# Two placements for the split weights of a column pair, and the order of their products

## The chip, the core and the metric

The kernel runs on one core of one Trainium2 chip. The metric is device time in microseconds of one execution. Engines by their names in the profile: PE (matrix products), PEld (loading of the stationary operand into PE), DVE (vector), ACT (scalar and activation), POOL, SP (here: issue of DMAs).

## The reference, cut to what matters

Two transformer blocks on 256 tokens of width 1024, all in float32. Block one: a modulated RMS norm, a mixer with three attention branches whose gated outputs are merged, and a convolutional feed-forward layer of width 2816. Block two: a gated linear attention layer, then a dilated sliding-window attention layer, each with a layer norm.

```python
z = h @ w_in                                    # q, k, v of three branches, gates zg
gates = jax.nn.sigmoid(zg.reshape(B_, S, 3, 1024) + b_gate)
merged = sum(gates[:, :, i] * (y_i @ w_branch[i]) for i in range(3))
x = x + g1 * _rmsnorm(merged @ w_out, ...)
a, g = jnp.split(h2 @ w_up, 2, axis=-1)         # feed-forward: 5632 columns
x = x + g2 * _rmsnorm((jax.nn.gelu(conv(a)) * g) @ w_down, ...)
q, k, v, g, a_lr = jnp.split(x @ gla_w_in, ...) # linear attention
k, v = jnp.split(x3 @ w_kv, 2, axis=-1)         # shared keys and values
q, g = jnp.split(x3 @ swa_w_in, [3072], axis=-1)
```

Every product is float32 x float32, and nearly all of the weights (some 35 million numbers) are used once, for all 256 tokens.

## The kernel before

**Products in three parts.** PE runs its fast float32 form (`F32R`) on operands that are split into a high and a low part. A weight piece of 128 x 1024 goes from HBM into a tile `raw` (DMA on SP's queue), ACT copies it to `whi` (line 158) and DVE writes the remainder into `wlo` (line 159). Activations are split in the same way (`hhi`/`hlo`, `h2hi`/`h2lo`, `x2hi`/`x2lo`, `x3hi`/`x3lo`). `mm3` (line 271) then issues three products into one accumulator: low weights with high activations, high weights with low activations, high with high. All of them are recorded at line 262.

**Two ways round.** In `tokmm` the activations are stationary and the weights stream by, 512 columns at a time; these chunks (`out`, `dn`, `gvg`, `gout`, `kvv`, `sout`) are not touched by the change. In `wpair` (line 522) and in the first loop (line 493) the weights are stationary and the 256 tokens stream by: each product loads one 128 x 128 block of weights and streams 128 x 256 of activations. A `wpair` chunk holds two column tiles of 128 outputs, each with 8 blocks along the contraction, so 2 x 8 x 3 = 48 products. Column tile 0 is the first piece of the chunk (`parts[0]`), column tile 1 the second; they go to the two halves of one PSUM tile. All of tile 0 comes first, then tile 1. `fresh` chunks (the first `up` and the first `kvk`) have an order of their own.

**Places in memory.** `whi` and `wlo` have six buffers each, so three chunks. A `whi` tile has 4096 bytes a partition; a `wlo` tile has 4224, and for the keys in `STILL` (all weights that are stationary) its data begins 64 bytes in. So high parts begin at 0 and low parts at 64 modulo 128, in both pieces. Activations lie in `big8` tiles (line 397), whose last argument shifts the data by that many floats: 0 for `hhi`, `hlo`, `x2hi`, `x2lo`, `h2hi`; 16 (64 bytes) for `h2lo`; 8 and 24 (32 and 96 bytes) for `x3hi` and `x3lo`.

**Order.** `Stream.get` (line 168) hands out a chunk and issues the DMA and the conversion of the chunk two further on; those pieces wait until their buffers are free, that is, until the last product that reads them is done. Each engine works off its instructions in order. That order is made when the program is built, by a list scheduler that takes what is ready by its own cost model and by priorities that follow the program (`tc.high_priority(n)` moves work ahead, `issue_after` holds it behind another instruction). So an edit can also move neighbours.

**Stages, in microseconds of the profile.** First projections `in1` (18 to 66); gates `zg` and branches `br` mixed with the three attentions (66 to 190); `out` (190 to 213); feed-forward `up` and `dn` (221 to 406); linear attention with `gla`, `gk` (410 to 438) and then `gvg`, `gout`; shared keys and values `kvk`, `kvv` (543 to 577); eight heads of window attention with two `sq` chunks each (577 to 703); the end. In `in1` each of eight steps holds 12 column tiles of one block, 8 in piece 0 and 4 in piece 1.

Of the kernel before, what the change touches and what calls it, by code (L numbers as in the profile page):

```python
# [20 lines left out]
KK = 8  # L21
# [11 lines left out]
SC_SWA = float(128.0 ** -0.5)  # L33


STILL = ("in1", "inc", "zg", "br", "up", "gla", "gk", "kvk", "sq")

COLS = {}

# [63 lines left out]
class Stream:  # L103
# [31 lines left out]
    def _chunk(self, i):  # L135
        nc = self.nc
        key, ap, n, part = self.items[i]
        if part < 0:
            raw = self.early.tile([128, n], F32, tag="early", name="early", bufs=3)
        else:  # L140
            raw = self._raw()
        if not part:
            for o in range(0, n, 1024):
                nc.sync.dma_start(raw[:, o:o + 1024], ap[:, o:o + 1024])
            self.done.append(raw)
            return
        nc.sync.dma_start(raw[:, :n], ap)
        parts = []
        for o in range(0, n, part) if part > 0 else range(0, -part, 1024):
            m = min(part, n - o) if part > 0 else min(1024, -part - o)  # L150
            hi = self.pool.tile([128, 1024], F32R, tag="whi", name="whi", bufs=self.hlbufs)
            lo = self.pool.tile([128, 1056], F32R, tag="wlo", name="wlo", bufs=self.hlbufs)
            lo = lo[:, 16:1040] if key[0] in STILL else lo[:, 0:1024]
            with ExitStack() as st:
                for ins in self.behind:
                    st.enter_context(self.tc.issue_after(ins))
                st.enter_context(self.tc.high_priority(self.pri))
                i0 = nc.scalar.activation(hi[:, :m], raw[:, o:o + m], AF.Copy)  # L158
                i1 = nc.vector.tensor_sub(lo[:, :m], raw[:, o:o + m], hi[:, :m].bitcast(F32))  # L159
                self.last = (i0.ins, i1.ins)  # L160
            parts.append((hi, lo))
        self.done.append((part, parts) if part > 0 else (raw, (1024, parts)))
# [36 lines left out]
def wsl(w, a, b):  # L199

    part, parts = w
    i = a // part
    assert b <= (i + 1) * part
    return tuple(t[:, a - i * part:b - i * part] for t in parts[i])
# [26 lines left out]
def hybrid_blocks(ctx, tc, A, out, dbg=None):  # L231
# [29 lines left out]
    def mm(o, l, r, start, stop, share=False):  # L261
        return pe.matmul(o, l, r, start=start, stop=stop, skip_group_check=share)  # L262
# [5 lines left out]
            st.enter_context(tc.issue_after(i))  # L268
        return st

    def mm3(o, l, r, start, stop, share=False):
        mm(o, l[1], r[0], start, False, share)
        mm(o, l[0], r[1], False, False, share)
        return mm(o, l[0], r[0], False, stop, share)

    def sl(pair, *ix):
        return tuple(t[ix] for t in pair)
# [215 lines left out]
    for j in range(KK):  # L493
        cur = h32
        ws.behind = at
        raw, w = ws.get(("in1", j), 1 if j + 1 < KK else None)
        if j + 1 < KK:
            h32, at = first_h(j + 1, gemv(ws.get(("ada", j + 1), 0))[0])
        h = sl(hT, slice(None), j, slice(None))
        for n in range(8):  # L500
            o = qk[n // 4][n % 4 // 2][:, (n % 2) * 256:(n % 2 + 1) * 256]
            mm3(o, wsl(w, n * 128, (n + 1) * 128), h, j == 0 and n % 2 == 0, j == KK - 1, True)
        for n in range(4):
            o = qci[n // 2][:, (n % 2) * 256:(n % 2 + 1) * 256]
            mm3(o, wsl(w, 1024 + n * 128, 1024 + (n + 1) * 128), h, j == 0 and n % 2 == 0, j == KK - 1, True)
        for b in range(2):
            mm(vps[b], cur[:, b * 128:(b + 1) * 128], raw[:, 1536:2048], j == 0, j == KK - 1)
    ws.pri = 0
# [8 lines left out]
    def wstat(o, w, base, a, share=False, kk=KK):  # L517
        for k in range(kk):
            mm3(o, wsl(w, base + k * 128, base + (k + 1) * 128), sl(a, slice(None), k, slice(None)),
                k == 0, k == kk - 1, share)  # L520

    def wpair(key, a, fresh=False):


        w = ws.get(key)
        p = mm_t()
        if fresh:
            for n in range(2):
                o = p[:, n * 256:(n + 1) * 256]
                W = [wsl(w, n * 1024 + k * 128, n * 1024 + (k + 1) * 128) for k in range(KK)]  # L530
                for k, l in enumerate(W):
                    mm(o, l[1], a[0][:, k, :], k == 0, False)
                    mm(o, l[0], a[0][:, k, :], False, False)
                for k, l in enumerate(W):
                    mm(o, l[0], a[1][:, k, :], False, k == KK - 1)
            return p
        for n in range(2):
            wstat(p[:, n * 256:(n + 1) * 256], w, n * 1024, a)
        return p

    def rope_pair(wk, tag, p, ctab, stab, half, dst, n=2, nb=2, scale=1.0):
# [360 lines left out]

    close_p1()
    close_p1a()
    res, _ = open_pool("res")
    ctx.callback(_)
    p2, close_p2 = open_pool("p2")
    wk = p2
    xn = p2.tile([128, 2, D], F32, name="xn")
# [281 lines left out]
    xqt = p3.tile([128, 2, D], F32, name="lnw", tag="sg")  # L1191
    layer_norm(x2, y3, row("lng0"), None, x3, lambda i: (xkt, xqt)[i // 2][:, i % 2, :], ORD3)
    dump("x3", x3)
    x3T = (big8(F32R, "x3hi", 8), big8(F32R, "x3lo", 24))

    def ev_x3(j, p, act, dve):
        for low in range(2):
# [16 lines left out]
            nc.scalar.dma_start(x3d[b], x3[:, b, :])  # L1214

    close_p3()
    p4, close_p4 = open_pool("p4")
    ctx.callback(close_p4)
    wk = p4
# [224 lines left out]
```

## Time and profile before

| | us |
|---|---|
| median of 3 runs | 741.2 (741.21, 735.28, 741.20) |
| the profiled execution | 733.62 |
| its span, first to last instruction | 731.6 |
| PE busy in the span | 700.6 (96%) |
| PEld busy | 636.4 (87%) |
| DVE busy | 547.1 (75%) |
| ACT busy | 407.1 (56%) |
| mean granted clock of PE | 0.986 |

A product's record on PE is longer than the distance to the next one, because products overlap in the pipeline; busy time of PE is the union of the records and therefore says only that PE had something under way. What a product costs in a stream is the distance from its start to the next start. In the rows, `mm<-x3hi,wlo` means that the moving operand is `x3hi`, the stationary one `wlo`, and the output a PSUM tile named `mm`.

### The profile page before, as it was taken

The page shows a single profiled execution, that of the slowest core. Times are in us where ns is not written, and L with a number is a line of the kernel's source. Part 1 is how long each engine was busy: PE and PEld are TensorE (multiplying, and loading weights), DVE is VectorE, ACT ScalarE, POOL GpSimd, SP SyncE. Part 2 cuts the span into 40 slices and gives each one's busy share as a digit, 9 for nine tenths or more (in the row PEclk, how much of TensorE's full clock was granted, in tenths as well). Part 3 has the DMA queues.
Part 4 walks back from the last instruction along what each step waited for, and adds up shares of the span by engine and source line. Part 5 has one row for each costly group of instructions (what it writes and reads, how often), then busy time and mean ns, then how long its engine had stood idle before and what let it go on. Part 6 is the DMA issues. An engine that isn't in the chain of part 4 may idle for free. (4 is left out here: it accounts for less than half of the span.)

```text
span 731.6 us, 12192 instructions
## 1 busy us (share of the span) xinstructions
PE 700.6 (96%) x4878; PEld 636.4 (87%) x4878; DVE 547.1 (75%) x933; ACT 407.1 (56%) x675; POOL 20.2 (3%) x34
## 2 busy tenths in 40 slices
PE   4999999999979999999999899999989999999995
PEld 4888888998859999998999797888879999999984
DVE  5877969898868776768566756675777689777866
ACT  3447788546548555554545774543555556555542
POOL 0001000000010000000000200001010000000000
PEclk8999999999999999999999999999999999999999
DMA  8996768677734765758554464231437755433201
GB/s 321 418 345 237 275 257 301 229 250 255 256 136 174 276 243 178 262 207 310 201 195 174 181 224 141 109 116 58 189 142 276 261 194 168 168 125 135 89 1 57
DMA packets 24600, 148.74 MB, mean 203 GB/s; under 512 B 2992, under 2 KB 3248, under 8 KB 9568
## 3 DMA queue, kind: packets, MB, share of 16 engines
q1 hardware_dynamic: 21888, 139.05, 52.1%
q0 software_dynamic: 1280, 5.18, 2.1%
q10 hardware_dynamic: 1376, 3.74, 1.5%
q8 instruction: 38, 0.62, 0.3%
q14 instruction: 18, 0.15, 0.1%
HBM read 145.86 MB, written 2.10 MB: 202 GB/s over the span
## 5 line engine op out<-in xcount | busy, mean ns | idle before, releaser
L159 DVE TENSOR_TENSOR wlo<-raw,whi 128x1024 fp32r<-128x1024 f32 (+1 forms) x193 | 231.3, 1210 | 63.1 <-ACT whi L158 63.1
L158 ACT ACTIVATE whi<-raw 128x1024 fp32r<-128x1024 f32 (+1 forms) x193 | 199.4, 1050 | 94.1 <-PE acc L262 42.5
L262 PE MATMUL mm<-h2hi,wlo 128*128 128x256 f32 x352 | 98.3, 280 | 0.0
L262 PE MATMUL mm<-h2hi,whi 128*128 128x256 f32 x352 | 98.1, 280 | 0.0
L262 PE MATMUL mm<-h2lo,whi 128*128 128x256 f32 x352 | 97.0, 282 | 0.0
L262 PE MATMUL mm<-x3hi,wlo 128*128 128x256 f32 x304 | 86.2, 285 | 0.0
L262 PE MATMUL mm<-x3hi,whi 128*128 128x256 f32 x304 | 85.1, 281 | 0.0
L262 PE MATMUL mm<-x3lo,whi 128*128 128x256 f32 x304 | 82.9, 280 | 0.0
L262 PEld LDWEIGHTS mm<-h2hi,wlo 128*128 128x128 f32 x352 | 67.0, 190 | 0.4
L262 PEld LDWEIGHTS mm<-h2hi,whi 128*128 128x128 f32 x352 | 66.9, 190 | 0.0
L262 PEld LDWEIGHTS mm<-h2lo,whi 128*128 128x128 f32 x352 | 65.1, 188 | 0.3
L262 PE MATMUL mm<-hhi,wlo 128*128 128x256 f32 x208 | 59.5, 286 | 0.5 <-DVE wlo L159 0.3
L262 PE MATMUL mm<-hlo,whi 128*128 128x256 f32 x208 | 59.2, 285 | 0.0
L262 PE MATMUL mm<-hhi,whi 128*128 128x256 f32 x208 | 58.7, 282 | 0.0
L262 PEld LDWEIGHTS mm<-x3hi,wlo 128*128 128x128 f32 x304 | 57.7, 190 | 0.0
L262 PEld LDWEIGHTS mm<-x3hi,whi 128*128 128x128 f32 x304 | 57.5, 189 | 0.0
L262 PEld LDWEIGHTS mm<-x3lo,whi 128*128 128x128 f32 x304 | 56.2, 188 | 0.0
L262 PEld LDWEIGHTS mm<-hhi,wlo 128*128 128x128 f32 x208 | 39.0, 188 | 2.5 <-PE mm L262 0.8
L262 PEld LDWEIGHTS mm<-hlo,whi 128*128 128x128 f32 x208 | 39.1, 188 | 0.8 <-issue 0.8
L262 PEld LDWEIGHTS mm<-hhi,whi 128*128 128x128 f32 x208 | 39.1, 188 | 0.6 <-issue 0.5
L445 DVE SCALAR_TENSOR_TENSOR adacc<-raw,cact,adacc 128x1024 f32<-128x1024 f32 x28 | 35.7, 1276 | 0.2
L262 PE MATMUL acc<-whi,flo 128*128 128x512 f32 x88 | 34.8, 395 | 0.0
(355 smaller groups left out, 1604.0 us busy)
## 6 DMA issues: line engine op xcount, KB each, us to landing
raw<-in_w_up_dram SPq DMA_DIRECT2D x22, 1024.0 KB, 4.9
raw<-in_w_ada_dram SPq DMA_DIRECT2D x16, 1024.0 KB, 4.9
raw<-in_swa_q_dram SPq DMA_DIRECT2D x16, 1024.0 KB, 4.9
raw<-in_w_zg_dram SPq DMA_DIRECT2D x12, 1024.0 KB, 4.9
raw<-in_w_dn_dram SPq DMA_DIRECT2D x11, 1024.0 KB, 4.7
raw<-in_w_ada_dram SPq DMA_DIRECT2D x16, 512.0 KB, 9.0
early<-in_w_in_dram SPq DMA_DIRECT2D x8, 1024.0 KB, 7.3
raw<-in_gla_vg_dram SPq DMA_DIRECT2D x8, 1024.0 KB, 5.1
```

The costliest lines, as they stand in the source:

```text
L158: i0 = nc.scalar.activation(hi[:, :m], raw[:, o:o + m], AF.Copy)
L159: i1 = nc.vector.tensor_sub(lo[:, :m], raw[:, o:o + m], hi[:, :m].bitcast(F32))
L262: return pe.matmul(o, l, r, start=start, stop=stop, skip_group_check=share)
L445: dve.scalar_tensor_tensor(a, w, c, a, op0=OP.mult, op1=OP.add)
```

## The change

`STILL` is split. For seven of its nine keys (`ALTERNATE`) the place now depends on the piece: in even pieces the high part begins at 0 and the low part at 64 modulo 128, in odd pieces it is the other way round. `whi` tiles grow to 4224 bytes for that. `br` and `gla` stay as they were. In `wpair`, apart from `fresh`, the loop over the two column tiles moves inside the loop over the contraction, and the three products of a block go as high weights with low activations, low weights with high activations, high with high (`turn`). The first loop takes its 12 column tiles in the order 0, 1, 2, 3, 4, 8, 5, 9, 6, 10, 7, 11, also with `turn`. `x3hi` and `x3lo` lose their shifts. The pool `res`, which holds `x2`, is closed before the pool `p4` of the last stage opens, rather than at the end.

```diff
--- before.py
+++ after.py
@@ -33,7 +33,9 @@
 SC_SWA = float(128.0 ** -0.5)
 
 
-STILL = ("in1", "inc", "zg", "br", "up", "gla", "gk", "kvk", "sq")
+
+ALTERNATE = ("in1", "inc", "zg", "up", "gk", "kvk", "sq")
+STILL = ALTERNATE + ("br", "gla")
 
 COLS = {}
 
@@ -148,9 +150,11 @@
         parts = []
         for o in range(0, n, part) if part > 0 else range(0, -part, 1024):
             m = min(part, n - o) if part > 0 else min(1024, -part - o)
-            hi = self.pool.tile([128, 1024], F32R, tag="whi", name="whi", bufs=self.hlbufs)
+            hi = self.pool.tile([128, 1056], F32R, tag="whi", name="whi", bufs=self.hlbufs)
             lo = self.pool.tile([128, 1056], F32R, tag="wlo", name="wlo", bufs=self.hlbufs)
-            lo = lo[:, 16:1040] if key[0] in STILL else lo[:, 0:1024]
+            odd = len(parts) % 2 if key[0] in ALTERNATE else 0
+            past = (16 * odd, 16 * (1 - odd)) if key[0] in STILL else (0, 0)
+            hi, lo = (t[:, p:p + 1024] for t, p in zip((hi, lo), past))
             with ExitStack() as st:
                 for ins in self.behind:
                     st.enter_context(self.tc.issue_after(ins))
@@ -268,10 +272,11 @@
             st.enter_context(tc.issue_after(i))
         return st
 
-    def mm3(o, l, r, start, stop, share=False):
-        mm(o, l[1], r[0], start, False, share)
-        mm(o, l[0], r[1], False, False, share)
-        return mm(o, l[0], r[0], False, stop, share)
+    def mm3(o, l, r, start, stop, share=False, turn=False):
+
+        for n, (i, j) in enumerate(((0, 1), (1, 0), (0, 0)) if turn else ((1, 0), (0, 1), (0, 0))):
+            ins = mm(o, l[i], r[j], start and n == 0, stop and n == 2, share)
+        return ins
 
     def sl(pair, *ix):
         return tuple(t[ix] for t in pair)
@@ -497,12 +502,9 @@
         if j + 1 < KK:
             h32, at = first_h(j + 1, gemv(ws.get(("ada", j + 1), 0))[0])
         h = sl(hT, slice(None), j, slice(None))
-        for n in range(8):
-            o = qk[n // 4][n % 4 // 2][:, (n % 2) * 256:(n % 2 + 1) * 256]
-            mm3(o, wsl(w, n * 128, (n + 1) * 128), h, j == 0 and n % 2 == 0, j == KK - 1, True)
-        for n in range(4):
-            o = qci[n // 2][:, (n % 2) * 256:(n % 2 + 1) * 256]
-            mm3(o, wsl(w, 1024 + n * 128, 1024 + (n + 1) * 128), h, j == 0 and n % 2 == 0, j == KK - 1, True)
+        for n in (0, 1, 2, 3, 4, 8, 5, 9, 6, 10, 7, 11):
+            o = (qk[n // 4] if n < 8 else qci)[n % 4 // 2][:, (n % 2) * 256:(n % 2 + 1) * 256]
+            mm3(o, wsl(w, n * 128, (n + 1) * 128), h, j == 0 and n % 2 == 0, j == KK - 1, True, True)
         for b in range(2):
             mm(vps[b], cur[:, b * 128:(b + 1) * 128], raw[:, 1536:2048], j == 0, j == KK - 1)
     ws.pri = 0
@@ -534,8 +536,10 @@
                 for k, l in enumerate(W):
                     mm(o, l[0], a[1][:, k, :], False, k == KK - 1)
             return p
-        for n in range(2):
-            wstat(p[:, n * 256:(n + 1) * 256], w, n * 1024, a)
+        for k in range(KK):
+            for n in range(2):
+                mm3(p[:, n * 256:(n + 1) * 256], wsl(w, n * 1024 + k * 128, n * 1024 + (k + 1) * 128),
+                    sl(a, slice(None), k, slice(None)), k == n == 0, k == KK - 1, True, True)
         return p
 
     def rope_pair(wk, tag, p, ctab, stab, half, dst, n=2, nb=2, scale=1.0):
@@ -902,8 +906,7 @@
 
     close_p1()
     close_p1a()
-    res, _ = open_pool("res")
-    ctx.callback(_)
+    res, close_res = open_pool("res")
     p2, close_p2 = open_pool("p2")
     wk = p2
     xn = p2.tile([128, 2, D], F32, name="xn")
@@ -1191,7 +1194,7 @@
     xqt = p3.tile([128, 2, D], F32, name="lnw", tag="sg")
     layer_norm(x2, y3, row("lng0"), None, x3, lambda i: (xkt, xqt)[i // 2][:, i % 2, :], ORD3)
     dump("x3", x3)
-    x3T = (big8(F32R, "x3hi", 8), big8(F32R, "x3lo", 24))
+    x3T = (big8(F32R, "x3hi"), big8(F32R, "x3lo"))
 
     def ev_x3(j, p, act, dve):
         for low in range(2):
@@ -1214,6 +1217,7 @@
             nc.scalar.dma_start(x3d[b], x3[:, b, :])
 
     close_p3()
+    close_res()
     p4, close_p4 = open_pool("p4")
     ctx.callback(close_p4)
     wk = p4
```

## Rows read from the trace of the kernel before

**Rows 1.** The page: its first line, and busy time, share of the span and instructions of PE and DVE.

```profile
span 731.6 us, 12192 instructions
PE 700.6 (96%) x4878; PEld 636.4 (87%) x4878; DVE 547.1 (75%) x933; ACT 407.1 (56%) x675; POOL 20.2 (3%) x34
```

**Rows 2.** The waits of PE: who waited for whom, us in total, times, longest. The first row is the longest of all; the second is the only one for weights.

```profile
PE acc L890 <- DVE x L193: 4.1, 3, 2.7
...
PE mm L262 <- DVE wlo L159: 0.3, 1, 0.3
```

**Rows 3.** Busy time by stage: stretch, its length, then busy us (and instructions) of PE, PEld, DVE, ACT, POOL, the granted clock, the share of the DMA engines and GB/s.

```profile
18.00:66.00 48.00, 48.00 (x317) 39.68 (x316) 38.76 (x73) 23.14 (x38) 1.65 (x3) 0.96 0.87 330
66.00:190.00 124.00, 121.26 (x992) 111.75 (x991) 111.58 (x232) 85.46 (x182) 2.01 (x3) 1.00 0.73 268
...
577.00:703.00 126.00, 125.98 (x995) 122.27 (x994) 100.51 (x185) 74.54 (x121) 0.00 (x0) 1.00 0.41 142
```

**Rows 4.** The chain that ended last, in order of time: start, us, what. The last stages, from 410 on; a piece of 48 is one `sq` chunk.

```profile
410.41 6.28 PE mm L262 x49
...
646.57 5.67 PE mm L262 x48
```

**Rows 5.** Groups of instructions by line and shape: the products of stationary weights with 256 tokens, one group of each three; count, busy us, mean ns of one record, idle before.

```profile
L262 PE MATMUL mm<-h2hi,wlo 128*128 128x256 f32 x352 | 98.3, 280 | 0.0
...
L262 PE MATMUL mm<-x3hi,wlo 128*128 128x256 f32 x304 | 86.2, 285 | 0.0
...
L262 PE MATMUL mm<-hhi,wlo 128*128 128x256 f32 x208 | 59.5, 286 | 0.5 <-DVE wlo L159 0.3 <-DVE st L674 0.2
...
L262 PE MATMUL mm<-x2hi,wlo 128*128 128x256 f32 x72 | 20.4, 284 | 0.0
```

**Rows 6.** Timeline of PE in a gate chunk: start, us of the record, what. Consecutive products; three rows are one block.

```profile
83.00 0.28 PE L262 MATMUL mm<-hlo,whi 128*128 128x256 f32 x1
83.12 0.28 PE L262 MATMUL mm<-hhi,whi 128*128 128x256 f32 x1
83.23 0.28 PE L262 MATMUL mm<-hhi,wlo 128*128 128x256 f32 x1
83.35 0.28 PE L262 MATMUL mm<-hlo,whi 128*128 128x256 f32 x1
83.47 0.28 PE L262 MATMUL mm<-hhi,whi 128*128 128x256 f32 x1
83.58 0.28 PE L262 MATMUL mm<-hhi,wlo 128*128 128x256 f32 x1
83.69 0.28 PE L262 MATMUL mm<-hlo,whi 128*128 128x256 f32 x1
```

**Rows 7.** Timeline of PE, first and last start of low weights with high activations in five stretches of back-to-back products: the `inc` chunk (15 such rows), a gate chunk (15), two `up` chunks (32), the second and third `gk` (19 of theirs), three of `sq` (46).

```profile
66.74 0.28 PE L262 MATMUL mm<-hhi,wlo 128*128 128x256 f32 x1
...
71.59 0.28 PE L262 MATMUL mm<-hhi,wlo 128*128 128x256 f32 x1
...
131.85 0.28 PE L262 MATMUL mm<-hhi,wlo 128*128 128x256 f32 x1
...
136.84 0.28 PE L262 MATMUL mm<-hhi,wlo 128*128 128x256 f32 x1
...
293.63 0.28 PE L262 MATMUL mm<-h2hi,wlo 128*128 128x256 f32 x1
...
304.39 0.28 PE L262 MATMUL mm<-h2hi,wlo 128*128 128x256 f32 x1
...
418.89 0.28 PE L262 MATMUL mm<-x2hi,wlo 128*128 128x256 f32 x1
...
425.24 0.28 PE L262 MATMUL mm<-x2hi,wlo 128*128 128x256 f32 x1
...
577.87 0.28 PE L262 MATMUL mm<-x3hi,wlo 128*128 128x256 f32 x1
...
593.79 0.28 PE L262 MATMUL mm<-x3hi,wlo 128*128 128x256 f32 x1
```

**Rows 8.** Timeline of PE in a `dn` chunk, the other way round (activations stationary, 512 columns of weights stream by): first and last of 8 starts of `wlo` with `fhi`, with two products between each.

```profile
288.40 0.40 PE L262 MATMUL acc<-wlo,fhi 128*128 128x512 f32 x1
...
293.18 0.39 PE L262 MATMUL acc<-wlo,fhi 128*128 128x512 f32 x1
```

**Rows 9.** Timelines of PE and DVE where a chunk starts before its second piece is converted: the first product of the gate chunk, then the conversion of its second low part. Two gate chunks; then the four low parts of `gk` 0 and 1 in one row.

```profile
107.10 0.38 PE L262 MATMUL mm<-hhi,wlo 128*128 128x256 f32 x1
...
108.43 1.22 DVE L159 TENSOR_TENSOR wlo<-raw,whi 128x1024 fp32r<-128x1024 f32 x1
...
156.15 0.35 PE L262 MATMUL mm<-hhi,wlo 128*128 128x256 f32 x1 [0.29 <-DVE wlo L159]
...
156.32 1.21 DVE L159 TENSOR_TENSOR wlo<-raw,whi 128x1024 fp32r<-128x1024 f32 x1
...
412.08 4.63 DVE L159 TENSOR_TENSOR wlo<-raw,whi 128x1024 fp32r<-128x1024 f32 x4
```

**Rows 10.** Timeline of ACT in the feed-forward: the high parts of the two pieces of `up` 11, each when its buffer comes free.

```profile
296.62 1.06 ACT L158 ACTIVATE whi<-raw 128x1024 fp32r<-128x1024 f32 x1 [1.73 <-PE mm L262]
...
299.86 1.05 ACT L158 ACTIVATE whi<-raw 128x1024 fp32r<-128x1024 f32 x1
```

## The prediction, made before the changed kernel ran

> **What bounds the kernel now.** I read the page first, then the waits of PE, then busy time by stage, then the chain. PE has something under way for 96% of the span, and DVE, the next engine, for 75% [rows 1]. The longest single wait of PE is 4.1 us in total, and for converted weights it waited once, 0.3 us [rows 2]. In the window attention PE is busy 125.98 of 126 us [rows 3], and the chain of work that ended last runs there through product after product, one `sq` chunk being 5.67 us of it [rows 4]. So from the feed-forward on, a shorter product is a shorter kernel. Two stages are less simple. In the first 18 to 66 us the DMA engines are 87% busy at 330 GB/s [rows 3]: weights arrive no faster than that, and what PE saves there it waits for again. From 66 to 190 us DVE is busy 111.58 of 124 us beside PE's 121.26 [rows 3], with the attentions' vector work and the conversions in one queue.
>
> Busy PE is not PE at its peak, so the question is what one product costs in a stream. I take distances between starts. In a gate chunk [rows 6] the step after low activations with high weights is 0.12 to 0.13 us (83.00, 83.35 and 83.69 to the next start), the other two kinds 0.11 to 0.12. All three stream 256 columns. A block of weights is loaded while the product before it streams (PEld is busy 636.4 us beside PE, [rows 1]). The long step is the one during which the next block lies at the same place modulo 128 as the block before it (high after high); during the other two the place changes. Over whole stretches [rows 7], three products take (71.59 - 66.74)/14 = 346 ns in the `inc` chunk, (136.84 - 131.85)/14 = 356 in a gate chunk, (304.39 - 293.63)/31 = 347 in `up`, (425.24 - 418.89)/18 = 353 in `gk` and (593.79 - 577.87)/45 = 354 in `sq`. Same instructions, same clock, two levels about 8 ns apart.
>
> **How low can it go?** The bound comes from `dn` [rows 8]: 21 products of 512 columns between 288.40 and 293.18, 227.6 ns each. There a load comes only once in 512 columns, and still a column costs the same as in the short steps above: half of 227.6 is 113.8, three times that 341.4. I take this as the floor of three products.
>
> One page of the Trainium skill would put it lower: "TensorE: Matmul & The Clock Gate" (section Back-to-back issue gap) gives columns over 2.4 GHz plus 2.5 ns, by my estimate 109 ns for 256 columns. No row here shows a product of this form that short, and by it the sum below would be some 12 us larger.
>
> **The change, part by part.**
>
> *Placement and turns.* High, low, high of one column tile now lie at 0, 64, 0, the next at 64, 0, 64, so each load changes place against the one before. If the reading above is right, all three products step at the floor. Triples per stage, from counts [rows 5]: `up` has 352, less 16 in the `fresh` chunk: 336 x (347 - 341.4) = 1.9 us. `sq` is 16 chunks, 256 triples of the 304: 256 x 12.6 = 3.2 us; two `kvk` chunks, 32 x 12.6 = 0.4 us. `gk` is 64 of the 72: 64 x 11.6 = 0.7 us. The gates and `inc` are 208, between the two levels; at their middle, 351, this is 208 x 9.6 = 2.0 us. Together 8.2 us. The bounds of this term: nothing below the floor, so 8.2 (9.2 if all gate chunks were at 356) is the top; at the bottom each step could become like the long one (0.123 by [rows 6], 370 ns per triple), bounded below under the rivals. I take the upper part, because the steps with changing places are short in [rows 6], which is the nearest row.
>
> *`in1`.* Its 96 triples are behind the DMA engines [rows 3]: nothing. If weights came early, the price would be 96 x 5 ns = 0.5 us.
>
> *Both pieces at the start.* Column tile 1's low part is now wanted at the fifth product, some 0.47 us into the chunk (four steps of 0.12), no longer after half of it (2.8 us by the 5.67 of [rows 4]). Where conversion is ahead this costs nothing. Where it is not [rows 9]: one gate chunk starts at 107.10 and its second low part is ready at 108.43 + 1.22 = 109.65, so PE would stand until then, 2.1 us; part of that is filled by score products that now follow, and I take 1.0. Another starts at 156.15, second low part ready 157.53: 0.9 us. `gk` 0 starts after the 24 `gla` products, near 413.2 [rows 4], with its second low part ready at 412.08 + 4.63/2 = 414.4: 0.7 us. Together 2.6; between 0 (the list scheduler puts other products there) and 3.7. Queued behind such a product are PE's attention products, and behind these ACT's and DVE's softmax.
>
> *Buffers come free later.* Piece 0 used to be released at half time: `up` 11's first high part starts 3.24 us before its second [rows 10]. Now both start at the end of a chunk. They are wanted two chunks later, more than 11 us (2 x 5.5) against 3.5 us of two ACT and two DVE conversions at 1.06 and 1.22 [rows 9, 10]: nothing, as long as the two engines are free. The cover is the third buffer; in the gates, where DVE is 90% busy, it may fail, which the 3.7 above includes.
>
> *Places of x3, larger `whi`, `res` closed early.* `x3hi` and `x3lo` at 0 are placed as `hhi` and `hlo`, whose chunks have shown both levels [rows 7]; no price of its own. The last stage's tiles move in memory; x2's last reader is the first layer norm, long before, so no new wait; I bound it by 0.5 us either way.
>
> **The sum.** 8.2 - 2.6 = 5.6, rounded up to 6 us for waits that the scheduler fills. The profiled execution took 733.62 us (span 731.6 and 2.0 around it), so some 727.7 there, 0.8% less. The median of the runs is 741.2, 1% above the profiled one; the same 0.8% makes 735.
>
> **Rivals.**
>
> *Place doesn't matter.* The two levels also occur with the same places: `hhi`, `hlo` in the two chunks of [rows 7], and `x2` is placed like `h` but stays at 353. So the level may be a rhythm between load and stream that any order can fall into. Then the triples stay where they are, and only the waits are left: 741.2 + 0 to 3.7, near 743. Against it: within one chunk the long step is always the same one [rows 6]. The Trainium skill's page "SBUF — State Buffer" (section SBUF: two separate sides) would have it so, since it gives PE one read port for the moving operand and a second, independent one for weights. Rows 6 do not agree with two ports that never meet.
>
> *The new order is worse.* Slower by this: the turns give load and stream no step in which they get clear of each other, and each step becomes the long one, 123 ns or 370 per triple. The `up` chunks, whose `h2lo` at 64 is placed for the old order, pay most: 336 x 23 = 7.7 us; `sq`, `kvk` and `gk` 352 x 16 = 5.6; the gates 208 x 19 = 4.0. That is 17 us and 758 at the extreme; it is slower by 1% from a mean of 362 per triple (896 triples, 8 ns more, 7.4 us). For it: no trace shows this order. Against it: even the worst stretch shows 356.
>
> *The floor is not one.* Steps fall under 113.8, to 110 say: 896 x 11 = 10 us more, 725. For it: the floor is read from another form. Against it: not one row below it.
>
> *Half of it.* Only activations at equal places gain, `up` stays at 347: 1.9 less, 737. It lies within the range.
>
> **Chances.** Forecast, a gain of 3.5 to 9 us (732 to 738, half of it included): 0.55. Place doesn't matter, within 1%: 0.22. Worse order: 0.14. No floor: 0.09. A difference of 1% (7.4 us) is about what a measurement of this kernel can tell from none, as its own three runs lie 0.8% apart. Faster by over 1% takes the whole of no-floor and two fifths of the forecast, as 8.2 us without waits is 1.1%: 0.09 + 0.22 = 0.31. Slower by over 1%: 0.14. Within: 0.55. The range leaves out the worse order beyond 744 and the far end of no-floor: 727 to 744.
>
> **What the profile after would show.** If right: in `sq` and `gk`, three products within 345 ns, the three kinds of step equal, a `sq` chunk near 5.45 us in the chain; in `up` the same or 347 still. DVE's low parts of odd pieces as PE's releaser in the gates, 1 to 3 us in all. ACT's two conversions back to back at a chunk's end in the feed-forward, with no wait of PE behind. It would be wrong if `sq` chunks stay at 5.67, or if the waits for `wlo` come to more than the products save.

## The result and the profile after

The changed kernel takes 744.5 us (median of 7 runs, 744.0 to 746.1) against 736.7 us (735.3 to 741.2) of the kernel before (median of 7 runs): a ratio of 1.0105, interval 1.008 to 1.013. It is slower by about 1%, where 735 us were predicted and a range of 727 to 744. The prediction counted from 741.2, the median of the three runs it had; in its own terms a gain of 6 us was forecast and a loss of 7.8 came. The profiled execution took 744.11 us with a span of 742.1, 10.5 us more than the span of before [rows 1].

The page of the kernel after, its first line and the busy times:

```profile
span 742.1 us, 12200 instructions
...
PE 706.3 (95%) x4878; PEld 641.1 (86%) x4878; DVE 545.2 (73%) x933; ACT 405.6 (55%) x675; POOL 20.2 (3%) x34
```

PE has the same 4878 product records and is busy 5.7 us longer. The other 4.8 us are gaps. Where the time is lost is seen from the start of each stage's unbroken run of products in the two timelines:

| starts at (us) | before | after | lost in the stage before it |
|---|---|---|---|
| `inc`, first gate products | 66.4 | 66.3 | -0.1 |
| `out` | 191.4 | 196.5 | 5.2 |
| `up` | 220.5 | 226.2 | 0.6 |
| x2 into `gla` | 410.4 | 419.0 | 2.9 |
| `kvk` | 542.8 | 551.5 | 0.1 |
| `sq` | 577.2 | 586.3 | 0.4 |
| `sout`, the end | 700.1 | 710.6 | 1.4 |

Three of them lost: the gates, the feed-forward and the window attention. The 0.6 us before `up` belong to the gates too: in the kernel before, two products of `out` ran early, at 189.4, which in the kernel after are still to be done at 196.5. For the gates and the window attention, the waits of PE in the kernel after (who waited for whom: us in total, times, longest), beside [rows 2]:

```profile
PE mm L266 <- DVE wlo L163: 3.7, 4, 1.8
...
PE mm L266 <- ACT th L747: 1.8, 2, 1.2
...
PE at L1286 <- DVE sP L1273: 1.0, 3, 0.3
```

The first row was 0.3 us before; the other two are new. Against them, two waits for `Pat` on ACT fell from 2.0 to 0.4 us. The longest wait in the timeline of the kernel after: PE's last product, DVE's conversion that it is waiting for, and the product that follows.

```profile
86.30 0.28 PE L266 MATMUL mm<-hlo,whi 128*128 128x256 f32 x1
...
87.08 1.22 DVE L163 TENSOR_TENSOR wlo<-raw,whi 128x1024 fp32r<-128x1024 f32 x1
...
88.36 0.44 PE L266 MATMUL mm<-hhi,wlo 128*128 128x256 f32 x1 [1.78 <-DVE wlo L163]
```

This is the low part of a second piece, wanted at the fifth product of a gate chunk, as the prediction said; only it is another chunk than the two it priced. Windows of the kernel after for the gates, for the window attention and for two short stretches inside the gates (columns as in [rows 3]; the granted clock is the third number from the end):

```profile
66.00:196.00 130.00, 124.37 (x997) 115.53 (x996) 112.35 (x232) 86.29 (x182) 2.02 (x3) 0.97 0.70 256
586.00:713.00 127.00, 126.04 (x993) 121.97 (x992) 98.56 (x183) 73.36 (x120) 0.00 (x0) 1.00 0.40 141
...
88.55:91.96 3.41, 3.41 (x18) 3.41 (x17) 2.74 (x11) 2.96 (x6) 0.00 (x0) 0.50 0.77 245
132.93:136.34 3.41, 3.41 (x18) 3.41 (x17) 3.41 (x8) 2.00 (x2) 0.00 (x0) 0.50 0.90 303
```

In the gates PE is without work for 5.6 of 130 us, after 2.7 of 124 [rows 3]. The granted clock is 0.97 there, after 1.00: in the two short stretches it is at the lower of its two levels, 1.2 GHz, and products step at 213 ns instead of 118, which loses some 1.7 and 1.5 us. The first begins right behind the wait above, the second with no wait of that length before it. The traces of `order_only` and `narrow_turns` below, which have the same turns, show both at the same points of the gates; that of the kernel before has none in the gates. But `x3_64` and `shift_128`, in the old order, have one each, near 134. So part of the gates' loss is clock, and the timed runs below measure waits and clock together.

For the feed-forward, the timeline of PE in the kernel after: the first and last of 32 starts of `wlo` with `h2hi` in two `up` chunks, and of 48 starts with `x3hi`, as in [rows 7].

```profile
283.64 0.28 PE L266 MATMUL mm<-h2hi,wlo 128*128 128x256 f32 x1
...
294.63 0.28 PE L266 MATMUL mm<-h2hi,wlo 128*128 128x256 f32 x1
...
586.43 0.28 PE L266 MATMUL mm<-x3hi,wlo 128*128 128x256 f32 x1
...
603.04 0.28 PE L266 MATMUL mm<-x3hi,wlo 128*128 128x256 f32 x1
```

(294.63 - 283.64)/31 = 354.5 ns per triple in `up`, 347 before: 336 x 7.5 = 2.5 of the 2.9 us; the rest is `dn`, whose three products went from 684 to 688 ns (88 x 4 ns = 0.4). (603.04 - 586.43)/47 = 353.4 in `sq`, 354 before. Nowhere do three products take 341. In the chain of waits a `sq` chunk has 5.66 us (5.67 in [rows 4]):

```profile
663.25 5.66 PE mm L266 x48
```

### The profile page after: what moved, and what is told of

The parts are those of the page before. It is cut to its first block, busy times and chain, and to the rows that moved or that the text cites. A ratio compares the mean times of both kernels' runs of the same rounds, so it can differ in the third digit from the quotient of the medians.

```text
span 742.1 us, 12200 instructions
## 1 busy us (share of the span) xinstructions
PE 706.3 (95%) x4878; PEld 641.1 (86%) x4878; DVE 545.2 (73%) x933; ACT 405.6 (55%) x675; POOL 20.2 (3%) x34
## 5 line engine op out<-in xcount | busy, mean ns | idle before, releaser
L266 PE MATMUL mm<-hlo,whi 128*128 128x256 f32 x208 | 61.6, 296 | 0.0
L266 PEld LDWEIGHTS mm<-hhi,wlo 128*128 128x128 f32 x208 | 40.6, 195 | 4.6 <-DVE wlo L163 4.1
```

## The experiments

In what follows `up`, `x2` and x3 stand for the mean triple in two `up` chunks, over the last 55 starts of `wlo` in `gk`, and in the first three chunks of `sq`, worked out from first and last starts as above. Ratios are against the kernel before, run beside each kernel on the same chip. The later groups rest on the addresses that the built program gives to the tiles; no trace shows them. In the kernel before, `whi` buffers lie 4096 bytes apart, all at 0 modulo 256. Its `wlo` buffers, 4224 bytes apart, put the low parts at 64 and 192 by turns, and its `up` chunks are at 347 with either. The two buffers of the activations lie at 0 (`hhi`, `h2hi`, `x2lo`, `x3hi`) and at 128 modulo 256 (`hlo`, `h2lo`, `x2hi`, `x3lo`), to which the shifts are added. Places modulo 128, as the section on the kernel before gives them, hide that.

### Streams by themselves

One kernel without loads or conversions in between: streams of 96 products each, in the orders and at the places modulo 128 of before and after, and some simpler ones.

```diff
+STREAMS = [
...
+    ('sa', 'tiles', (0, 16, 0, 16), (0, 0)),
...
+    ('sg', 'turns', (0, 16, 16, 0), (0, 16)),
...
+    ('sj', 'turns', (0, 16, 0, 16), (0, 16)),
...
+    ('tc', 'w_alt', (0, 16, 0, 0), (0, 0)),
...
+]
```

> Leaves out the whole of the blocks: 26 streams of 96 products each, nothing else (and two to warm up), and zeros come out. Each stream has its own order and places, so that the distance between starts can be read for each without waits. Theory A (place of the load against the load before decides): the turns with alternating places (sf, sg, sh, uf, ug) step at 114 ns, tiles with places 0/64 (sa, sb, sc) at 116 with the long step at high after high, all at one place (sd, se) at 120; w_alt (tc) 114, same (ta) 120. Theory B (a rhythm of load and stream that does not hang on the load before, but on where the moving data begin against the load): then tc and ta are equal or differ by the activations' place alone (ta against tb, te against tf), and the turns show 118 wherever the activations lie, as in the changed kernel.

Timeline of PE, first and last of 32 starts of `wlo` with the high activations in `sa` (order and places of before, activations as in the gates) and `sj` (order of after at the old places, activations as in `up`), and of 48 in `tc` (weights at 0 and 64 by turns, one activation):

```profile
36.06 0.28 PE L94 MATMUL sa<-ahi,wlo 128*128 128x256 f32 x1
...
46.81 0.28 PE L94 MATMUL sa<-ahi,wlo 128*128 128x256 f32 x1
...
137.52 0.27 PE L94 MATMUL sj<-ahi,wlo 128*128 128x256 f32 x1
...
148.67 0.28 PE L94 MATMUL sj<-ahi,wlo 128*128 128x256 f32 x1
...
228.53 0.28 PE L94 MATMUL tc<-ahi,wlo 128*128 128x256 f32 x1
...
239.61 0.28 PE L94 MATMUL tc<-ahi,wlo 128*128 128x256 f32 x1
```

`sa` takes 10.75/93 = 115.6 ns per product, with steps of 114, 120 and 113; `sj` 11.15/93 = 119.9, where the old order with the same activations (`sb`) has 115.6; `tc`, where every load changes place against the one before, 11.08/94 = 117.9. `sg`, the order and places of the change, has 118.9. Over all streams the means run from 115.6 to 120.0; only the old order with weights at 0 and 64 and high activations at 0 has 115.6, and none has 113.8. Four of them, run a second time, settled at the same means. So the reading that the change rests on (theory A) falls: loads that change place are not short as such, and the short steps of 113 in `sa` are only had beside one of 120. Theory B as written falls too: `ta` and `tc` have the same activation and differ (119.9 and 117.9), and the turns are not all at 118 but run from 116.7 to 119.9 by the places.

### Order alone and places alone

The changed kernel with the places modulo 128 of before (`order_only`):

```diff
-            odd = len(parts) % 2 if key[0] in ALTERNATE else 0
+            odd = 0
```

> The new order (turns, low between) with the places of before (high at 0, low at 64 in both pieces); x3 unshifted and res closed early as in the change. If the order alone does it (the turns cost the fast level, and both pieces are wanted at the start): 1.008 to 1.012 of the kernel before, up triples near 354, waits for wlo 3 to 4 us. If the new places are the cause: up triples back at 347 and 1.004 to 1.007 (the waits alone remain).

The changed kernel with the order of before in `wpair` and in the first loop (`place_only`):

```diff
-        for k in range(KK):
-            for n in range(2):
-                mm3(p[:, n * 256:(n + 1) * 256], ..., k == n == 0, k == KK - 1, True, True)
+        for n in range(2):
+            for k in range(KK):
+                mm3(p[:, n * 256:(n + 1) * 256], ..., k == 0, k == KK - 1, False, False)
```

> The new places (odd pieces the other way round) with the order of before, x3 unshifted, res closed early. If the order alone does it: 0.998 to 1.002, up triples 347 in both pieces, waits for wlo under 1 us. If the places are the cause: odd pieces step at 354, up +1 to +2 us, ratio 1.003 to 1.006.

`order_only`: 1.0115 (1.0063 to 1.0166), `up` 353.3, `wlo` waits 3.6 us. `place_only`: 1.0044 (1.0019 to 1.0069), `up` 354.3, `wlo` waits 0.2 us. Each part alone is a loss, where each expectation set one of the two against the other, and the two do not add up to the whole. In `place_only` the two column tiles differ; timeline of an `up` chunk, starts of `wlo` with `h2hi`: the first of tile 0, the first of tile 1 and the last (eighth) of tile 1.

```profile
285.60 0.27 PE L266 MATMUL mm<-h2hi,wlo 128*128 128x256 f32 x1
...
288.37 0.28 PE L266 MATMUL mm<-h2hi,wlo 128*128 128x256 f32 x1
...
290.89 0.28 PE L266 MATMUL mm<-h2hi,wlo 128*128 128x256 f32 x1
```

Tile 0 takes 2.77/8 = 346 ns per triple, tile 1 2.52/7 = 360. The swapped places lose the rhythm of the old order.

### Low activations at 64

The kernel before with `hlo` and `x2lo` at 64, x3 at 0 and 64 (`low_acts_64`), as `h2` is placed:

```diff
-    hT = (big8(F32R, "hhi"), big8(F32R, "hlo"))
+    hT = (big8(F32R, "hhi"), big8(F32R, "hlo", 16))
...
-    x2T = (big8(F32R, "x2hi"), big8(F32R, "x2lo"))
+    x2T = (big8(F32R, "x2hi"), big8(F32R, "x2lo", 16))
...
-    x3T = (big8(F32R, "x3hi", 8), big8(F32R, "x3lo", 24))
+    x3T = (big8(F32R, "x3hi"), big8(F32R, "x3lo", 16))
```

> The kernel before with the low activations of h, x2 and x3 at 64 modulo 128, as h2lo has it already, and the high ones at 0. If the place of the low activations is what keeps up at 347 while x2 and x3 sit at 353: gk, kvk and sq triples fall to 347 (352 triples x 7 ns = 2.4 us) and the gate chunks all to 347 (208 x 4 = 0.9 us): ratio 0.994 to 0.997. If the level is a rhythm that place does not steer: triples stay, ratio 0.999 to 1.001.

0.9983 (0.9958 to 1.0008), between the two expectations and not told from 1: x3 went to 346.9, `x2` to 356.8, and the triples of `in1` from 348 to 356. The same places modulo 128 gave different things. x3 alone so placed (`x3_64`, the last line of the diff):

> The kernel before, with only `x3hi` at 0 and `x3lo` at 64 (before: 32 and 96); `hlo` and `x2lo` stay at 0. With all three low tiles moved, the triples of x3 went from 353.9 to 349.0 ns, those of `x2` from 353.4 to 355.9, and the whole was 0.9983 of before. Theory (level set by order and places together): x3 is at 349 again, x2 at 353.4; 304 triples x 4.9 ns = 1.5 us less, 0.998 of before. Rival: a gain of the sq stage is given back by its vector and scalar work (DVE is busy 80% of it), or x3 is at 354 because the place of the tiles before it shifts other tiles: no difference, 1.000.

x3 at 346.9, `x2` at 353.5 as expected, but 0.9991 (0.9969 to 1.0014): the timed runs do not tell the gain from none.

### The gates in the old order

The changed kernel, `inc` and `zg` chunks one column tile after the other as before (`gates_old`):

```diff
...
+        for n, k in [(n, k) for n in range(2) for k in range(KK)] if key[0] in ("inc", "zg") else [(n, k) for k in range(KK) for n in range(2)]:
+            old = key[0] in ("inc", "zg")
+            mm3(p[:, n * 256:(n + 1) * 256], wsl(w, n * 1024 + k * 128, n * 1024 + (k + 1) * 128),
+                sl(a, slice(None), k, slice(None)), k == 0 and (old or n == 0), k == KK - 1, not old, not old)
```

> The changed kernel, with the order of before (column tile 0, then column tile 1; low weights, low activations, high) given back to the gate chunks and the `inc` chunk alone. The changed kernel lost 5.1 us between 66 us and the start of `out`. Theory of the waits: there the low part of the second piece is wanted at the fifth product, before DVE has it, and PE's queue stands with attention work behind it. Then the old order gives back 4 to 5 us (start of `out` at 191.5 to 192.5, after 196.5; the whole near 740), the waits of PE for `wlo` fall from 3.7 us to under 1, while `up` stays at 354 to 355 ns per triple. Rival, the length of the products: the gate triples went from 350.6 to 353.5 ns, 208 of them are 0.6 us, and that is all that comes back: `out` at 196, the whole at 744. Second rival, the granted clock: half-rate stretches of 3.4 us in the gates come without regard to the order; then the loss stays where such stretches stay.

And all chunks tile after tile, only the order inside a block new (`low_between`):

```diff
-        for k in range(KK):
-            for n in range(2):
+        for n in range(2):
+            for k in range(KK):
...
-        for n in (0, 1, 2, 3, 4, 8, 5, 9, 6, 10, 7, 11):
+        for n in range(12):
```

> The changed kernel, with column tile 0 before column tile 1 again in all chunks (no turns of the two tiles) and the first loop's 12 tiles in their old order; the order inside a block stays new (low part between the high ones), and so do the new places. Theory (the level is set by order and places together): the order inside a block alone loses the fast rhythm, as the streams with old places showed 117.7 and 119.8 ns for it: `up` at 353 to 358 ns per triple in both halves of a chunk. The waits of the gates, that come from wanting both pieces at once, go: `out` at 191.5 to 192.5. Together 739 to 741. Rival, the turns alone cost the rhythm: then the first half of each `up` chunk (even piece, old places) is at 347 and only the second at 361, as with the new places in the old order, and the whole at 739 too, so that the two halves of the chunk decide, not the time.

`gates_old`: 1.0043 (1.0022 to 1.0064), `out` starts at 192, `up` stays at 354.6. Its waits of PE for weights and for the window attention:

```profile
PE at L1286 <- DVE sP L1273: 1.0, 3, 0.3
...
PE mm L266 <- DVE wlo L163: 0.5, 1, 0.5
```

The row for `th` is gone. The trace still has one half-rate stretch in the gates, at 92.5, behind a wait of 2.4 us for `Pat` on ACT, so the rival of the clock is not wholly out.

`low_between`: 1.0029 (1.0011 to 1.0048), `up` 354.0 (355 to 356 in the first half of a chunk, 352 to 353 in the second: neither is at 347), both rows are gone from its list of waits, and its gates have no half-rate stretch. So the turns of the two tiles, with the waits and the clock that they bring, cost 1.0105 - 1.0043 = 0.6% (4.6 us) in the gates and 1.0105 - 1.0029 = 0.8% (5.6 us) in all. Each difference is uncertain by some 0.3%, so the runs do not tell the two apart; that the window attention has its share rests on the 1.0 us for `sP`. The remaining 0.3% fit the longer products of `up`.

### The size of the tiles

Every kernel so far with a slow `up` also had the wider `whi` tiles. The kernel before with that alone, and `res` closed early to make room (`wide_whi`):

```diff
-            hi = self.pool.tile([128, 1024], F32R, tag="whi", name="whi", bufs=self.hlbufs)
+            hi = self.pool.tile([128, 1056], F32R, tag="whi", name="whi", bufs=self.hlbufs)
...
+            hi = hi[:, 0:1024]
```

> The kernel before, with `whi` tiles of 4224 bytes instead of 4096 whose data begins at 0 as before, and `res` closed early (without that the tiles of the last stage do not fit): only the sizes of the change, neither its places nor its order. `dn`, which the change does not touch, went from 684 to 688 ns per triple in all three kernels with wide `whi` tiles, and the `gout` chunks from 687 to 692.7. Theory: that is the new distance of the buffers from each other, so `dn` and `gout` are at 688 and 692.7 here too; it is 88 x 4 ns and 32 x 6 ns, 0.5 us in all, and the whole is within 0.3% of before. Rival: it follows from the order of the stationary products beside it; then 684 and 687. If `up` leaves 347 here, distances of whole multiples of 128 bytes matter as well, and place modulo 128 is not the whole description.

1.006 (1.0031 to 1.0088), where 0.3% at most were expected: beside the 1.05% of the whole change, from 128 unused bytes in each buffer. Two `up` chunks, as in [rows 7]:

```profile
280.15 0.28 PE L263 MATMUL mm<-h2hi,wlo 128*128 128x256 f32 x1
...
291.14 0.28 PE L263 MATMUL mm<-h2hi,wlo 128*128 128x256 f32 x1
```

10.99/31 = 354.5 ns, with the order of before and its places modulo 128. Buffers 4224 bytes apart lie at 0 and 128 modulo 256 by turns. The same with the data of every other buffer moved by 128 bytes, so that all are at 0 modulo 256 again (`wide_even`):

```diff
-            hi = hi[:, 0:1024]
+            buf = int(("054132" * 8 + "054321" * 99)[self.made])
+            self.made += 1
+            hi = hi[:, 32 * (buf % 2):32 * (buf % 2) + 1024]
```

> The kernel before with `whi` tiles of 4224 bytes (and `res` closed early), but the data in every other buffer begins 128 bytes in, so that all high parts begin at the same place modulo 256, as they do with tiles of 4096. With the wide tiles alone every other buffer lay at 128 modulo 256 and the whole was 1.006 of before. Theory: places count modulo 256, not 128, so this undoes the loss: `up` at 347, `dn` at 684, the whole within 0.2% of before. Rival: the distance of the buffers or the sheer size is the cause: `up` stays at 354, `dn` at 688 to 690, the whole at 1.004 to 1.006.

```profile
277.54 0.28 PE L266 MATMUL mm<-h2hi,wlo 128*128 128x256 f32 x1
...
288.30 0.28 PE L266 MATMUL mm<-h2hi,wlo 128*128 128x256 f32 x1
```

10.76/31 = 347.1 and 1.000 (0.998 to 1.002): all of it is back, also `dn` (684 ns per triple; 690 with the wide tiles alone). Not the size, but the place modulo 256; and closing `res` early, which this kernel has too, costs nothing. Last, all weights moved by 128 against the activations by longer `raw` tiles in front of them (`shift_128`):

```diff
-        return self.pool.tile([128, 2048], F32, tag="raw", name="raw", bufs=self.rawbufs)
+        return self.pool.tile([128, 2080], F32, tag="raw", name="raw", bufs=self.rawbufs)[:, 0:2048]
```

> The kernel before with `raw` tiles of 8320 bytes (and `res` closed early), which moves all high and low weight parts by 128 modulo 256 against the activations and leaves the distances between them alone. Theory: what counts is the place of the weights against the activations: `up` leaves 347 for 353 to 356, where the wide tiles showed the buffers at 128; `x2`, whose high activations lie at 128, is the one that may gain (350); the whole 1.003 to 1.005. Rival: it is enough that all buffers lie at one place: `up` stays at 347 and the whole at 1.000.

Two `up` chunks, then first and last of 55 starts of `wlo` with `x2hi`:

```profile
281.35 0.28 PE L262 MATMUL mm<-h2hi,wlo 128*128 128x256 f32 x1
...
292.44 0.29 PE L262 MATMUL mm<-h2hi,wlo 128*128 128x256 f32 x1
...
426.71 0.28 PE L262 MATMUL mm<-x2hi,wlo 128*128 128x256 f32 x1
...
445.50 0.28 PE L262 MATMUL mm<-x2hi,wlo 128*128 128x256 f32 x1
```

`up` goes from 347 to 11.09/31 = 357.7, `x2` from 353.4 to 18.79/54 = 348.0, the whole to 1.005 (1.0034 to 1.0066). The gates, whose high activations lie at 0 like those of `up`, went the same way (350.6 to 353.6). What counts in the old order is the place of the weights against the activations: the stage whose high weights and high activations lie at the same place modulo 256 is the fast one, and it can be chosen.

### The order alone, at the old sizes

With tiles and places of before, the new order alone (`narrow_turns`), as in the diff of the change:

> The kernel before with the new order alone (turns of the two column tiles, low part between the high ones, the first loop's order): places, tile sizes, `res` and x3 as before. Until now every kernel with the new order also had the wider `whi` tiles, and wider tiles alone (order and places modulo 128 as before) took `up` from 347 to 354.5 ns per triple. Theory A: the order has no fast rhythm at these places, whatever the tiles: `up` at 353 to 359 (the streams with this order and these places took 119.8 ns per product, 359 per triple), the gates lose 4 to 5 us by waits, the whole 743 to 747. Theory B: the size of the tiles was the whole cause of the longer products and the order costs waits alone: `up` at 347, the whole near 741.

1.0118 (1.0098 to 1.0139), and two `up` chunks at 11.13/31 = 359.0 ns:

```profile
284.93 0.28 PE L262 MATMUL mm<-h2hi,wlo 128*128 128x256 f32 x1
...
296.06 0.28 PE L262 MATMUL mm<-h2hi,wlo 128*128 128x256 f32 x1
```

The new order loses the rhythm at the good places too. Once it is lost, the new places and sizes have little left to spoil, which would explain why 1.2%, 0.4% (or 0.6%) and the 1.05% of the whole do not add.

### A kernel that beats both

The kernel before with x3 and `x2` placed modulo 256 as its own fast stages are (`best`):

```diff
-    x2T = (big8(F32R, "x2hi"), big8(F32R, "x2lo"))
+    x2T = (big8(F32R, "x2hi", 32), big8(F32R, "x2lo", 32))
...
-    x3T = (big8(F32R, "x3hi", 8), big8(F32R, "x3lo", 24))
+    x3T = (big8(F32R, "x3hi"), big8(F32R, "x3lo", 16))
```

> The kernel before with activations placed modulo 256 where its own fast stretches have them: `x3hi` and `x3lo` at 0 and 192 as `h2hi`, `h2lo` (in place of 32 and 224), `x2hi` and `x2lo` at 0 and 128 as `hhi`, `hlo` (in place of 128 and 0). Theory: x3 at 349 and `x2` at 348 to 350 ns per triple, both after 353.5: (304 x 4.6 + 72 x 4.5) ns = 1.7 us less, 0.9975 of before. Rival: `x2` does not follow the pattern, x3 alone gains 1.4 us, 0.998; or the gain drowns in the differences between executions in the gates, 1.000.

0.9973 (0.995 to 0.9996), just clear of 1, 735.4 us beside 737.1; the span of its profile is 729.7. First and last of 55 starts for `x2` and of 48 for x3:

```profile
418.60 0.28 PE L262 MATMUL mm<-x2hi,wlo 128*128 128x256 f32 x1
...
437.44 0.28 PE L262 MATMUL mm<-x2hi,wlo 128*128 128x256 f32 x1
...
576.40 0.28 PE L262 MATMUL mm<-x3hi,wlo 128*128 128x256 f32 x1
...
592.70 0.28 PE L262 MATMUL mm<-x3hi,wlo 128*128 128x256 f32 x1
```

348.9 and 346.8 ns, after 353.4 and 353.7. Over all 16 `sq` chunks x3 is at 349, as expected, because four of them stay at 353.5 to 354.2 at the same places.

The kernels side by side (places of `whi` modulo 256 in `up`; "mixed" is the new places on wide tiles):

| kernel | order | `whi` for `up` (`h2hi` at 0) | `up` ns | `x2` ns | x3 ns | ratio |
|---|---|---|---|---|---|---|
| before | old | 0 | 347.1 | 353.4 | 353.7 | 1 |
| `best` | old | 0 | 347.1 | 348.9 | 346.8 | 0.9973 |
| `wide_even` | old | 0 | 347.1 | 353.6 | 353.7 | 1.000 |
| `wide_whi` | old | 0, 128 | 354.5 | 353.5 | 354.4 | 1.006 |
| `shift_128` | old | 128 | 357.7 | 348.0 | 354.7 | 1.005 |
| `place_only` | old | 0, 192 | 354.3 | 352.0 | 354.7 | 1.0044 |
| `low_between` | tiles old, parts new | mixed | 354.0 | 352.1 | 353.1 | 1.0029 |
| `gates_old` | new but in the gates | mixed | 354.6 | 353.4 | 353.4 | 1.0043 |
| `narrow_turns` | new | 0 | 359.0 | 355.4 | 353.3 | 1.0118 |
| `order_only` | new | 0, 128 | 353.3 | 355.9 | 355.4 | 1.0115 |
| after | new | mixed | 354.5 | 353.2 | 353.4 | 1.0105 |

## Why the prediction was wrong

*What bounds the kernel* was right (its "longest single wait" of 4.1 us is three waits by [rows 2], which changes nothing): PE's longer triples and PE's gaps became time nearly one to one. By the traces the triples come to 2.5 us in `up` and 0.6 in the gates, and the gaps grew by 4.8: 7.9 of the 10.5 us between the two profiled executions, and the half-rate stretches (3.2 by their steps) about make up the rest. Both signs of being wrong that it named were seen: `sq` chunks stay at 5.66, and the waits cost more than the products save.

*Placement and turns*, the main term, failed in its sign: 8.2 us of gain were forecast, 2 to 3 us of loss came. Two steps of it were wrong. First, the long step was put down to a load at the same place as the load before it. [Rows 6] fit that, but they fit as well that the product with the low activations is long; alternating loads by themselves took 117.9 ns. One stretch in which two things always go together cannot tell them apart. Nor is the long step always the same one, as the prediction has it against its first rival: [rows 6] come from a chunk near the fast level, and in the slow chunk at 131.4 the three steps are at 118, 119 and 119. Second, the floor of 113.8 for all three steps was taken from another form of product, which loads once in 512 columns. At the fast level only two of three steps are near it, and no stream or column tile came under 115.4 on average (346 per triple). The bottom bound (each step 123 ns, 370 per triple) was wide enough; the choice of its upper part was the error.

*The larger `whi`* had no price of its own; with the places of x3 and `res` it stood at half a microsecond either way. Alone it measured 0.6% (0.3 to 0.9), some 4 us, though beside the new order it adds nothing (`narrow_turns` without it is at 1.0118). The step that failed here is "at 0 modulo 128" as the description of a place: the 128 bytes more put every other buffer at another place modulo 256, and `wide_even` and `shift_128` show that this is what counts.

*Both pieces at the start* was the right mechanism, mis-sized: 2.6 us, 3.7 at most, against 4.6 in the gates by `gates_old` and 5.6 in all by `low_between`. The price summed the pieces that would have been late in the old schedule; the waits for `wlo` themselves came to 3.7 us, its upper bound. It left out two things. One is the clock: a half-rate stretch follows the longest wait and loses some 1.7 us, and the second loses 1.5. How much of the timed 4.6 us is clock stays open. The other is the products' consumers: with turns both halves of a PSUM tile are done only at a chunk's end, and so the gates' `th` on ACT and the heads' `sP` on DVE start later and PE waits for them (1.8 and 1.0 us, rows of the result; the first is gone in `gates_old`, the second in `low_between`). The wait at `gk` 0 came nearly as priced: 0.5 us for `wlo`, where 0.7 was said.

*`in1`* at nothing and *buffers free later* at nothing held: `inc` starts at 66.3 after 66.4, although the triples of `in1` went from 348 to 353 ns, and PE has no wait for weights in the feed-forward.

*The rivals.* "The new order is worse" came true, with a chance of 0.14, though not by its price: triples did not go to 362 but to 354, and waits made up the rest. It had `up` paying most, which is what happened. "Place doesn't matter" is refuted by `shift_128`: one move by 128 bytes made one stage slower and another faster. Its thought of a rhythm is not: the same addresses show both levels (last section). The Trainium skill's page "SBUF — State Buffer" (section SBUF: two separate sides) says that PE never waits on anyone at its ports. These runs show that the places of PE's own two operands set its pace (347.1 against 357.7 in `shift_128`); that it is the reads which wait, they do not show. The gap of the Trainium skill's page "TensorE: Matmul & The Clock Gate" (section Back-to-back issue gap), 109 ns by the estimate in the prediction, is given there for a product by itself; no stream here reached it, the lowest mean being 115.6.

## What to carry over

Where a loop of equal products has several speeds, first write down the real addresses of all operands, and at a fine enough modulus: a buffer that grows by a few bytes moves all its neighbours, and may cost more than the edit it was made for. Before a rule is read from a stretch of steps, find a stretch where its two candidates come apart, or time a bare stream of them. And when two halves of a result are interleaved, price both ends: the inputs are wanted earlier, and the consumers of the first half start later.

## What the runs showed of the hardware

For this form (128 x 128 weights, 256 columns, the old order, low weights 64 modulo 128 off the high ones), a triple takes about 347 to 349 ns in most stretches where high weights and high activations lie at the same place modulo 256, and 351 to 361 where they do not. Over the eight traces in the old order, by the addresses of the built programs: of 270 column tiles at different places none is under 351 ns, and of 417 at the same place 350 are under 349. The streams agree: high activations at 32 or 64 against high weights at 0 (`sc`, `sm`) take the old order from 115.6 to 117.6 and 117.8 per product. They add that low weights at the place of the high ones modulo 128 (`sd`) take it to 117.9.

The same place is no guarantee. In the kernel before itself, four of the 13 `inc` and gate chunks, with both at 0, are at 354 to 356 (one is in [rows 7]). In `wide_whi` one buffer at 0 stays at 358.6 ns per triple, in `place_only` the same buffer, order and places run at 346.8. The two differ in what ran just before, so it seems that a slow rhythm can be carried on into a piece that would be fast by itself; no run tests this alone. The first chunk after `dn` also needs some ten products to settle, with single steps up to 127 ns (`wide_whi`, `place_only`; 124 before). Which part of the chip sets the rhythm no run here shows. Whether the new order has a fast set of places of its own is open: none of the seven streams with turns came under 116.7.
